# Transposes held back until a group's full-precision products, in a two-layer hybrid decoder

## The chip, the cores and the metric

The kernel runs on one core of a Trainium2 chip, in one launch. The metric is the device time in microseconds, the median of the runs shown. The core has five engines that each work through a queue of their own: TensorE (PE; its weight loads are shown as PEld), VectorE (DVE), ScalarE (ACT), GpSimd (POOL) and SyncE (SP, which here only issues DMAs). Matrix products are written to PSUM, in banks of 128 partitions by 512 fp32 numbers.

## What is computed

A trunk of two layers on 512 tokens with 1024 channels. The parts that matter here:

```
x  <- x + 1/2 SwiGLU_1(RMSNorm(x))
h   = RMSNorm(x)
[q|k|v|z|xBC|dt|g_sb|g_ssm] = h @ W_in
y_sb  = StickBreakingAttention(q,k,v) @ W_branch_sb
y_ssm = Mamba2_SSD(z,xBC,dt) @ W_branch_ssm      # 24 heads x 64 in 8 groups, state 128, chunks of 128
x  <- x + (sigmoid(g_sb)*y_sb + sigmoid(g_ssm)*y_ssm) @ W_out
x  <- x + 1/2 SwiGLU_2(RMSNorm(x))

ssd, per chunk:  cb = c_k b_k^T ;  y = (cb * decay) xdt + c_k state * exp(cum)
                 state <- state * exp(cum_end) + b_k^T (to_end * xdt)
```

## The kernel before, in words

Nearly all of TensorE's work are dense products in which both operands are split into a high and a low part of reduced precision, three matmuls for one (`mm3`, lines 315 to 317). Weights are fetched by SyncE, their high part is cast by ScalarE (line 282), the low part is subtracted by VectorE (line 284), two units ahead of the product that uses them. The dense results rotate through four PSUM banks (pool `pmm`, names `mm`).

The state-space part runs beside the dense products of the mixer. For each of its eight groups, and each of the four chunks c in a group, there are three tasks. `prepare(c)` makes decays on ScalarE (lines 1129 and 1131) and scaled inputs on GpSimd. `inner(c)` multiplies c by b (line 1140) and, except in the last chunk, makes the state's addend (line 1142), both in full precision into a bank of the pool `ptr` (two banks, names `pt`). `outer(c)` multiplies the decayed scores by the inputs (line 1157) and c by the state (line 1159), in full precision into a bank of the pool `pa` (two banks). Inner c+1 and outer c stand together.

The order is written by a clock of ticks: one or two steps of a dense product, of three matmuls each, make a tick, and each task is a generator that runs a step, says how many ticks to sleep, and goes on. What a task issues stands in the engines' queues at that tick. `ssd_group` (from line 1087) starts the chunks `PITCH` = 5 ticks apart.

Blocks have to be transposed between token rows and channel rows. `transposed` (line 849) does three or four 128x128 transposes on TensorE in full precision, each into a quarter of a bank:

- `conv_block` transposes the blocks x (named `cv`) and b (named `bT`) into a bank of `ptr`; ScalarE copies them out (lines 1053 and 1061).
- the end of `ssd_group` transposes the normed result of each group (named `raw`) and, after every second group, a tail of both (named `acc`) into a bank of `pa`; ScalarE takes the high part out (line 1223) and VectorE the low part (line 1225), both named `yt`.

The z products (`by_tokens`, 128x384) fill the four dense banks at once; `z_part` empties each by ScalarE (line 1082) and VectorE (line 1084).

Of the kernel before, what the change touches and what calls it, by code (L numbers as in the profile page):

```python
# [84 lines left out]
def conv_at(kind, i):  # L85

    if kind == "x":
        return OFF_X + i * P, i * TAPS
    at = (OFF_B, OFF_C)[kind == "c"] + i * P
    return at, (DIN // P + GROUPS * (kind == "c") + i) * TAPS  # L90
# [63 lines left out]
def all_units():  # L154
    table, off = {}, 0
    for layer in range(DEPTH):
        for key, n in unit_order(layer):
            table[key] = (off, n)
            if "pair" not in key or key[-1] in STORED:
                off += n * P * P  # L160
    return table, off


class Builder:
# [7 lines left out]
    def __init__(self, ctx, tc, xT, wflat, par, taps, out):  # L172
        self.tc, self.nc = tc, tc.nc
        self.ctx = ctx
        self.xT, self.wflat, self.par, self.taps, self.out = xT, wflat, par, taps, out
        self.units, _ = all_units()
        self.keys = list(self.units)
        self.pos = 0
        self.raw, self.loaded = [], []
        self.count = 0  # L180
        self.side = []
        self.xd = None
        self.sums, self.early, self.summed = {}, {}, 0
        for i, key in enumerate(self.keys):
            if key[2:] == ("gate", 0):
                first = i + 4
            if "pair" in key and key[-1] in ("s1", "s3"):
                self.early.setdefault(max(first, i - (5 if key[-1] == "s1" else 4)), []).append(key)
        self.logs = True

    def name(self, s):
        self.count += 1
        return f"{s}_{self.count}"
# [12 lines left out]
        self.side.append([gen, wait])  # L206

    def tick(self):
        for task in list(self.side):
            task[1] -= 1  # L210
            if task[1] <= 0:
                try:
                    task[1] = next(task[0])
                except StopIteration:
                    self.side.remove(task)
# [573 lines left out]
    def dt_stage(self, layer, ps):  # L789
# [56 lines left out]
        self.give("raw", "raw", "cv", "cv")  # L846
        self.dt_done = True

    def transposed(self, src, n=NT, aside=False):

        pt = self.t(self.pa, [P, SEQ], "pa") if aside else self.t(self.ptr, [P, SEQ], "pt")
        for c in range(n):
            cs = slice(c * P, (c + 1) * P)
            self.nc.tensor.transpose(pt[:, cs], src[:, cs], self.ident)  # L854
        return pt[:, :n * P].rearrange("p (c d) -> p c d", d=P)
# [160 lines left out]
    def conv_block(self, kind, i, ps):  # L1016


        nc, mp = self.nc, self.mp
        r = yield from self.take("raw")  # L1020
        u = yield from self.take("cv")
        _, k0 = conv_at(kind, i)
        tap = [self.conv[:, k0 + j:k0 + j + 1] for j in range(TAPS)]
        nc.scalar.activation(u, ps, AF.Identity, scale=tap[KCONV - 1], bias=tap[KCONV])  # L1024
        yield 2
        for j in range(1, KCONV):
            nc.vector.scalar_tensor_tensor(u[:, j:], ps[:, :SEQ - j], tap[KCONV - 1 - j], u[:, j:],  # L1027
                                           op0=ALU.mult, op1=ALU.add)
            yield 1
        yield 1  # L1030
        yield from self.opened()
        nc.scalar.activation(r, u, AF.Tanh)
        yield 1
        if self.cumb is None:
            self.load_cum(0)
        dst = u
        if kind != "x":
            dst = self.ssm[i][kind] = self.t(mp, [P, SEQ], kind + "T")
        nc.vector.scalar_tensor_tensor(dst, r, 1.0, u, op0=ALU.add, op1=ALU.mult)
        yield 3  # L1040
        if kind == "x":
            p, i = divmod(i, 3)
            pt = self.transposed(dst)
            yield 1
            for g in (2 * p, 2 * p + 1):
                a, b = max(i * P, g % 2 * GW), min((i + 1) * P, (g % 2 + 1) * GW)
                if a < b:
                    if "x" not in self.ssm[g]:
                        while not self.room["xs"]:
                            yield 1  # L1050
                        self.room["xs"] -= 1
                        self.ssm[g]["x"] = self.t(mp, [P, NT, GW], "xs", bufs=3)
                    nc.scalar.activation(self.ssm[g]["x"][:, :, a - g % 2 * GW:b - g % 2 * GW],
                                         pt[:, :, a - i * P:b - i * P], AF.Copy, scale=0.5)
                    self.ssm[g]["x", i] = True
            yield 1
        elif kind == "b":
            pt = self.transposed(dst, NT - 1)
            yield 1
            tok = self.t(mp, [P, NT - 1, P], "btok")  # L1060
            nc.scalar.copy(tok, pt)
            self.ssm[i]["btok"] = tok
        self.give("raw", "cv")
# [28 lines left out]
    def ssd_group(self, layer, g):  # L1092
# [15 lines left out]
        def heads(ap):  # L1108
            return ap.rearrange("p (h d) -> p h d", d=HD)

        def wide(ap):
            return ap.unsqueeze(2).to_broadcast([P, HPG, HD])

        def col(band, c):
            return tok[:, c, 32 * band + h0:32 * band + h0 + HPG]

        def span(c):
            return slice(c * P, (c + 1) * P)

        def prepare(c):  # L1120
            dec = decs[c] = self.t(mp, [P, HPG, P], "dec")
            x = heads(xs[:, c, :])
            if c < NT - 1:
                xws[c] = self.t(mp, [P, HPG, HD], "xw")
                nc.gpsimd.tensor_tensor(xws[c], x, wide(col(3, c)), op=ALU.mult)
            xdts[c] = self.t(mp, [P, HPG, HD], "xdt")
            nc.gpsimd.tensor_tensor(xdts[c], x, wide(col(0, c)), op=ALU.mult)
            for i in range(HPG):
                nc.scalar.activation(dec[:, i, :], cumb[:, i, span(c)], AF.Relu, scale=-1.0,
                                     bias=tok[:, c, 32 + h0 + i:33 + h0 + i])  # L1130
            nc.scalar.activation(dec, dec, AF.Exp, scale=-1.0)
            yield 1
            nc.gpsimd.affine_select(out=dec, in_=dec, pattern=[[0, HPG], [1, P]], compare_op=ALU.is_ge, fill=0.0,
                                    base=0, channel_multiplier=-1)
            nc.gpsimd.tensor_tensor(heads(y[:, c, :]), x, wide(par[:, G_D + h0:G_D + h0 + HPG]), op=ALU.mult)
# [42 lines left out]
            finished.append(c)  # L1178

        self.spawn(prepare(0))  # L1180
        yield 3
        self.spawn(inner(0))
        self.spawn(prepare(1))
        for c in range(NT):
            yield self.PITCH
            if c < NT - 1:
                self.spawn(inner(c + 1))
            self.spawn(outer(c))
            if c + 2 < NT:
                self.spawn(prepare(c + 2), 1)  # L1190
            elif c + 2 == NT and g < GROUPS - 1:
                yield 1
                self.load_cum(g + 1)
# [20 lines left out]
            todo.append((tail, 3 * (g // 2) + 2))  # L1214
        for src, blk in todo:
            yield 4
            pt = self.transposed(src.rearrange("p c d -> p (c d)"), aside=True).rearrange("p c d -> p (c d)")
            if src is yn:
                self.give("raw")
            yield 1  # L1220
            gain = par[:, G_SSM + blk:G_SSM + blk + 1]
            hi, lo = self.pair(self.yt, ("yt", "yt"))
            nc.scalar.activation(hi, pt, AF.Copy, scale=gain)
            yield 1
            nc.vector.scalar_tensor_tensor(lo, pt, gain, hi.bitcast(F32), op0=ALU.mult, op1=ALU.subtract)
            self.y_ssm[blk] = (hi, lo)
# [297 lines left out]
```

## Time and profile before

| | |
|---|---|
| three runs | 2598.34, 2594.51 and 2594.2 us; median 2594.51 |
| profiled execution | 2594.82 us, span 2593.0 us |
| TensorE busy | 2575.7 us (99%), 15074 matmuls |
| VectorE, ScalarE, GpSimd busy | 1761.2 us (68%), 1279.6 us (49%), 492.1 us (19%) |
| chain that ended last | TensorE 93%, VectorE 4%, ScalarE 2% |

The share of TensorE is its modelled busy time; since matmuls overlap, the distance between two starts tells more than the length of a row. A timeline row has the start, the length, the engine, the line, the operation, what it writes and reads and the shape; in brackets stand the idle time of the engine before it and who ended it. A full-precision matmul counts as two instructions there.

### The profile page before, as it was taken

What the parts mean: (1) busy time and instruction counts of PE and PEld (TensorE: products, weight loads), DVE (VectorE), ACT (ScalarE), POOL (GpSimd) and SP (SyncE); (2) the same over time, 40 slices, a digit from 0 to 9 for tenths busy, and PEclk for the clock granted to TensorE, in tenths of its full rate; (3) what the DMA queues carried; (4) which work ended last, traced back from release to release, by engine and by line L of the source; (5) the groups of instructions that cost most, each with busy time, mean ns of one, the idle gap of its engine ahead of it and who ended that gap; (6) DMA issues with size and microseconds to landing.
All of it is one profiled execution on the core that took longest, in us unless ns stands there. A gap on an engine that the chain in (4) does not pass through costs nothing.

```text
span 2593.0 us, 38317 instructions
## 1 busy us (share of the span) xinstructions
PE 2575.7 (99%) x15074; PEld 2300.5 (89%) x15074; DVE 1761.2 (68%) x2422; ACT 1279.6 (49%) x2101; POOL 492.1 (19%) x617
## 2 busy tenths in 40 slices
PE   9999999999999999999999999999999999999998
PEld 7898988888888889899998989888888888899997
DVE  7575876676664478585885858766676644776766
ACT  6343456655554255343553535566555533543444
POOL 0121201133242002021111312011333310021110
PEclk9999999999999999999999999999999999999999
DMA  5455442333333546473554645423333335464642
GB/s 189 137 147 146 122 139 76 102 114 101 109 104 106 163 140 169 131 187 108 161 142 127 173 129 130 137 74 113 101 102 104 113 112 160 139 182 128 175 121 78
DMA packets 105156, 336.35 MB, mean 130 GB/s; under 512 B 12256, under 2 KB 15584, under 8 KB 104976
## 3 DMA queue, kind: packets, MB, share of 16 engines
q1 hardware_dynamic: 93168, 293.46, 35.4%
q0 software_dynamic: 10944, 39.85, 8.7%
q8 instruction: 118, 1.93, 0.3%
q10 hardware_dynamic: 864, 0.60, 0.1%
q14 instruction: 62, 0.51, 0.1%
HBM read 321.18 MB, written 12.68 MB: 129 GB/s over the span
## 4 chain that ended last, share of the span: by engine, by line
PE 93%; DVE 4%; ACT 2%; DMA 1%; issue 1%; SPq 0%; DVEq 0%; ACTq 0%
PE mm L315 26%; PE mm L317 26%; PE mm L316 26%; PE pa L316 3%; PE pa L317 3%; PE pa L315 3%; PE pa L1157 2%; DVE wlo L284 1%; PE pa L1159 1%; PE pt L854 1%; PE pt L1142 1%; DMA wraw<-in_wflat_dram 1%; PE pt L1140 1%; ACT whi L282 1%; PE pa L968 0%
## 5 line engine op out<-in xcount | busy, mean ns | idle before, releaser
L282 ACT CAST whi<-wraw 128x1024 fp32r<-128x1024 f32 (+2 forms) x442 | 435.8, 986 | 604.3 <-PE mm L317 492.0
L284 DVE TENSOR_TENSOR wlo<-wraw,whi 128x1024 fp32r<-128x1024 f32 (+2 forms) x442 | 542.0, 1226 | 168.6 <-ACT whi L282 167.5
L315 PE MATMUL mm<-hhi,whi 128*128 128x512 f32 (+1 forms) x1600 | 571.9, 357 | 0.0
L316 PE MATMUL mm<-hhi,wlo 128*128 128x512 f32 (+1 forms) x1600 | 559.1, 349 | 2.1 <-DVE wlo L284 2.1
L317 PE MATMUL mm<-hlo,whi 128*128 128x512 f32 (+1 forms) x1600 | 559.7, 350 | 0.4 <-DVE hlo L504 0.4
L317 PEld LDWEIGHTS mm<-hlo,whi 128*128 128x128 f32 x1600 | 302.8, 189 | 40.9 <-DVE hlo L504 0.8
L316 PEld LDWEIGHTS mm<-hhi,wlo 128*128 128x128 f32 x1600 | 303.3, 190 | 39.4 <-DVE wlo L284 3.4
L315 PEld LDWEIGHTS mm<-hhi,whi 128*128 128x128 f32 x1600 | 303.2, 190 | 35.8 <-issue 1.0
L617 POOL TENSOR_TENSOR g<-g,rs 128x512 f32<-128x512 f32 x76 | 133.0, 1749 | 876.4 <-DVE g L624 855.4
L284 DVE TENSOR_TENSOR wlo<-s,whi 128x1024 fp32r<-128x1024 f32 x152 | 235.3, 1563 | 58.6 <-ACT whi L282 58.6
L315 PE MATMUL mm<-act,whi 128*128 128x512 f32 (+1 forms) x710 | 274.0, 386 | 0.0
L316 PE MATMUL mm<-act,wlo 128*128 128x512 f32 (+1 forms) x710 | 273.8, 386 | 0.0
L317 PE MATMUL mm<-act,whi 128*128 128x512 f32 (+1 forms) x710 | 273.6, 385 | 0.0
L315 PE MATMUL mm<-th,whi 128*128 128x256 f32 x912 | 258.1, 283 | 0.0
L316 PE MATMUL mm<-th,wlo 128*128 128x256 f32 x912 | 258.1, 283 | 0.0
L317 PE MATMUL mm<-tl,whi 128*128 128x256 f32 x912 | 258.1, 283 | 0.0
L282 ACT CAST whi<-s 128x1024 fp32r<-128x1024 f32 x152 | 158.8, 1045 | 103.3 <-PE mm L317 61.2
L643 DVE SCALAR_TENSOR_TENSOR x<-mm,x 128x512 f32<-128x512 f32 x93 | 64.1, 689 | 196.1 <-PE mm L317 196.1
L315 PEld LDWEIGHTS mm<-th,whi 128*128 128x128 f32 x912 | 175.1, 192 | 0.0
L316 PEld LDWEIGHTS mm<-th,wlo 128*128 128x128 f32 x912 | 175.1, 192 | 0.0
L317 PEld LDWEIGHTS mm<-tl,whi 128*128 128x128 f32 x912 | 175.1, 192 | 0.0
L1027 DVE SCALAR_TENSOR_TENSOR cv<-mm,conv,cv 128x511 f32<-128x511 f32 x168 | 125.1, 744 | 47.9 <-ACT cv L1024 46.3
(297 smaller groups left out, 5030.0 us busy)
## 6 DMA issues: line engine op xcount, KB each, us to landing
wraw<-in_wflat_dram SPq DMA_DIRECT2D x330, 512.0 KB, 3.7
s<-in_wflat_dram SPq DMA_DIRECT2D x76, 512.0 KB, 4.6
s<-in_wflat_dram POOLq DMA_DIRECT2D x76, 512.0 KB, 9.3
wraw<-in_wflat_dram SPq DMA_DIRECT2D x96, 384.0 KB, 3.1
cumb<-cum_d SPq DMA_DIRECT2D x16, 768.0 KB, 4.3
xd<-x SPq DMA_DIRECT2D x16, 256.0 KB, 3.2
wraw<-in_wflat_dram SPq DMA_DIRECT2D x16, 256.0 KB, 3.2
x<-xd SPq DMA_DIRECT2D x16, 256.0 KB, 5.3
```

The lines of the kernel that those rows point to most:

```text
L282: nc.scalar.copy(hi[:, :n], raw[:, :n])
L284: nc.vector.tensor_tensor(lo[:, :n], raw[:, :n], hi[:, :n].bitcast(F32), op=ALU.subtract)
L315: mm(ps, a[0], b[0], start=start, stop=False, **kw)
L316: mm(ps, a[1], b[0], start=False, stop=False, **kw)
L317: mm(ps, a[0], b[1], start=False, stop=stop, **kw)
L617: eng.tensor_tensor(r, r, self.rs[:, cols].unsqueeze(1).to_broadcast([P, 2, half]), op=ALU.mult)
L643: self.nc.vector.scalar_tensor_tensor(x, pd, 0.5, x, op0=ALU.mult, op1=ALU.add)
L854: self.nc.tensor.transpose(pt[:, cs], src[:, cs], self.ident)
L1027: nc.vector.scalar_tensor_tensor(u[:, j:], ps[:, :SEQ - j], tap[KCONV - 1 - j], u[:, j:], op0=ALU.mult, op1=ALU.add)
L1140: nc.tensor.matmul(pc[:, :P], bt[:, span(c)], ct[:, span(c)], start=True, stop=True)
L1142: nc.tensor.matmul(pu, btok[:, c, :], xws[c].rearrange("p h d -> p (h d)"), start=True, stop=True)
L1157: nc.tensor.matmul(py[:, i * HD:(i + 1) * HD], decs[c][:, i, :], xdts[c][:, i, :], start=True, stop=True)
```

## The change

Two methods are added. `due(ticks)` notes the tick at which a group's next full-precision products will be issued; `ssd_group` calls it before each sleep. `together(tag)` holds a task back: as long as a noted tick still lies ahead, it lets one transposing task for each tag (`pt` for the x and b blocks, `pa` for raw and tail) through at a noted tick, in which the products' tasks are later in the list, and makes it sleep otherwise. Where no noted tick lies ahead, it does nothing. The tasks that wait keep their room in the pools.

```diff
+        self.now, self.joined = 0, {}
...
     def tick(self):
+        self.now += 1
...
+    def together(self, tag):
+        while self.joined and self.now < max(self.joined):
+            if tag not in self.joined.get(self.now, (tag,)):
+                self.joined[self.now] += (tag,)
+                return
+            yield 1
+
+    def due(self, ticks):
+        self.joined[self.now + ticks] = ()
...
         if kind == "x":
             p, i = divmod(i, 3)
+            yield from self.together("pt")
             pt = self.transposed(dst)
...
         elif kind == "b":
+            yield from self.together("pt")
             pt = self.transposed(dst, NT - 1)
...
         self.spawn(prepare(0))
+        self.due(4)
         yield 3
         self.spawn(inner(0))
         self.spawn(prepare(1))
         for c in range(NT):
+            self.due(self.PITCH + 1)
             yield self.PITCH
...
         for src, blk in todo:
             yield 4
+            yield from self.together("pa")
             pt = self.transposed(src.rearrange("p c d -> p (c d)"), aside=True).rearrange("p c d -> p (c d)")
```

In the order that comes of it, 18 groups of transposes stand elsewhere on TensorE (one x block, four b blocks, two raw blocks and two tails in each layer), and with them their readers on ScalarE and VectorE; SyncE and GpSimd have the same order as before. The lines of the changed kernel are up to 20 higher.

TensorE before, in the second layer, at the tail of the second pair of groups (`pa_19594`), the second product group behind it (`pt_19608` is inner 1, `pa_19613` outer 0):

```order
L854 MATMUL pa_19594<-ident,acc_19025 128x128 x4
L315 MATMUL mm_19459<-whi_19476,hhi_15893 128x384
L316 MATMUL mm_19459<-whi_19476,hlo_15894 128x384
L317 MATMUL mm_19459<-wlo_19477,hhi_15893 128x384
L1140 MATMUL pt_19608<-cT_19329,bT_19240 128x128
L1142 MATMUL pt_19608<-xw_19562,btok_19291 128x192
L1157 MATMUL pa_19613<-xdt_19522,dec_19519 128x64 x3
```

TensorE after, at the same tail (now `pa_19647`), one product group further on (`pt_19652` is inner 2, `pa_19657` outer 1):

```order
L319 MATMUL mm_19459<-wlo_19539,hhi_15900 128x384
L869 MATMUL pa_19647<-ident,acc_19025 128x128 x4
L1157 MATMUL pt_19652<-cT_19329,bT_19240 128x128
L1159 MATMUL pt_19652<-xw_19610,btok_19327 128x192
L1174 MATMUL pa_19657<-xdt_19560,dec_19557 128x64 x3
L1176 MATMUL pa_19657<-state_19556,cT_19329 128x192
```

The tail has moved past inner 1 and outer 0, and so its `pa` bank is taken after outer 0's and not before.

ScalarE before, from the raw block's copy (`yt_19549`) and the tail's (`yt_19605`) to the first z activation:

```order
L1223 ACTIVATE yt_19549<-pa_19536,par_107 128x512
L1129 ACTIVATE dec_19561<-cumb_19363,sq_16580 128x128 x3
L1131 ACTIVATE dec_19561<-dec_19561 128x384
L282 CAST whi_19599<-wraw_19457 128x1024
L1223 ACTIVATE yt_19605<-pa_19594,par_107 128x512
L1129 ACTIVATE dec_19617<-cumb_19363,sq_16580 128x128 x3
L1131 ACTIVATE dec_19617<-dec_19617 128x384
L1129 ACTIVATE dec_19666<-cumb_19363,sq_16580 128x128 x3
L1131 ACTIVATE dec_19666<-dec_19666 128x384
L282 CAST whi_19673<-wraw_19531 128x1024
L1082 ACTIVATE z_19690<-mm_19459 128x384
```

ScalarE after, the same stretch:

```order
L1146 ACTIVATE dec_19557<-cumb_19363,sq_16580 128x128 x3
L1148 ACTIVATE dec_19557<-dec_19557 128x384
L1243 ACTIVATE yt_19572<-pa_19547,par_107 128x512
L284 CAST whi_19594<-wraw_19457 128x1024
L1146 ACTIVATE dec_19609<-cumb_19363,sq_16580 128x128 x3
L1148 ACTIVATE dec_19609<-dec_19609 128x384
L1146 ACTIVATE dec_19662<-cumb_19363,sq_16580 128x128 x3
L1148 ACTIVATE dec_19662<-dec_19662 128x384
L284 CAST whi_19669<-wraw_19531 128x1024
L1243 ACTIVATE yt_19675<-pa_19647,par_107 128x512
L1099 ACTIVATE z_19690<-mm_19459 128x384
```

The raw block's copy stands behind the decays of chunk 1, and the tail's copy behind the decays of chunks 2 and 3 and a weight cast, directly ahead of the z activations.

VectorE after, from the product that inner 2 feeds to the z products (before, the tail's `yt` stood ahead of inner 1's, and the y, t, weight and z operations followed `state` directly):

```order
L1165 TENSOR_TENSOR dec_19609<-pt_19652,dec_19609 128x384
L1169 TENSOR_TENSOR state_19655<-pt_19652,state_19655 128x192
L1245 SCALAR_TENSOR_TENSOR yt_19676<-pa_19647,par_107,yt_19675 128x512
L1179 TENSOR_TENSOR y_19513<-pa_19657,y_19513 128x192
L1182 TENSOR_TENSOR t_3314_19687<-pa_19657,sq_16580 128x192
L286 TENSOR_TENSOR wlo_19670<-wraw_19531,whi_19669 128x1024
L1101 SCALAR_TENSOR_TENSOR z_19690<-z_19690,mm_19459 128x384
```

VectorE before, the same stretch:

```order
L1148 TENSOR_TENSOR dec_19617<-pt_19656,dec_19617 128x384
L1152 TENSOR_TENSOR state_19659<-pt_19656,state_19659 128x192
L1162 TENSOR_TENSOR y_19513<-pa_19661,y_19513 128x192
L1165 TENSOR_TENSOR t_3314_19687<-pa_19661,sq_16580 128x192
L284 TENSOR_TENSOR wlo_19674<-wraw_19531,whi_19673 128x1024
L1084 SCALAR_TENSOR_TENSOR z_19690<-z_19690,mm_19459 128x384
```

The tail's low half has moved in behind inner 2's state, ahead of outer 1's y and t, the low half of a weight and the z products.

## Rows read from the trace of the kernel before

**Rows 1.** The page, busy us, share of the span and instructions of each engine.

```profile
PE 2575.7 (99%) x15074; PEld 2300.5 (89%) x15074; DVE 1761.2 (68%) x2422; ACT 1279.6 (49%) x2101; POOL 492.1 (19%) x617
```

**Rows 2.** Waits of TensorE at transposes: us in total, times, longest us.

```profile
PE pt L854 <- DVE cv L1039: 1.2, 6, 0.2
```

**Rows 3.** Timeline of TensorE around a lone x block: start us, length us.

```profile
1801.68 0.39 PE L317 MATMUL mm<-hlo,whi 128*128 128x512 f32 x1
1801.91 0.60 PE L854 MATMUL pt<-ident,cv 128*128 128x128 f32 x4
1802.27 0.48 PE L315 MATMUL mm<-hhi,whi 128*128 128x512 f32 x1
...
1802.81 0.40 PE L317 MATMUL mm<-hlo,whi 128*128 128x512 f32 x1
```

**Rows 4.** The same around a raw block that already stands in front of products.

```profile
545.16 0.39 PE L317 MATMUL mm<-hlo,whi 128*128 128x512 f32 x1
...
545.84 0.39 PE L317 MATMUL mm<-hlo,whi 128*128 128x512 f32 x1
546.07 0.60 PE L854 MATMUL pa<-ident,raw 128*128 128x128 f32 x4
...
547.53 0.40 PE L317 MATMUL mm<-hlo,whi 128*128 128x512 f32 x1
```

**Rows 5.** The same around the first two products of a group alone.

```profile
516.19 0.39 PE L317 MATMUL mm<-hlo,whi 128*128 128x512 f32 x1
...
517.42 0.39 PE L317 MATMUL mm<-hlo,whi 128*128 128x512 f32 x1
```

**Rows 6.** TensorE at the tail shown above: its transposes, outer 2, the next unit.

```profile
1952.88 0.60 PE L854 MATMUL pa<-ident,acc 128*128 128x128 f32 x4
...
1963.60 0.78 PE L1157 MATMUL pa<-xdt,dec 128*128 128x64 f32 x6
...
1965.12 0.39 PE L315 MATMUL mm<-hhi,whi 128*128 128x512 f32 x1
```

**Rows 7.** ScalarE in the same stretch.

```profile
1952.39 1.05 ACT L282 CAST whi<-wraw 128x1024 fp32r<-128x1024 f32 x1 [1.88 <-PE mm L316]
1953.52 0.69 ACT L1223 ACTIVATE yt<-pa,par 128x512 fp32r<-128x512 f32 x1
...
1960.07 0.99 ACT L1129 ACTIVATE dec<-cumb,sq 128x128 f32<-128x128 f32 x3 [3.31 <-PE pa L1157]
...
1961.52 1.04 ACT L282 CAST whi<-wraw 128x1024 fp32r<-128x1024 f32 x1
1962.47 1.24 ACT L1082 ACTIVATE z<-mm 128x384 f32<-128x384 f32 x3
```

**Rows 8.** VectorE in the same stretch.

```profile
1954.24 0.75 DVE L1225 SCALAR_TENSOR_TENSOR yt<-pa,par,yt 128x512 fp32r<-128x512 f32 x1 [2.39 <-ACT yt L1223]
1954.91 1.22 DVE L284 TENSOR_TENSOR wlo<-wraw,whi 128x1024 fp32r<-128x1024 f32 x1
...
1961.56 0.34 DVE L1162 TENSOR_TENSOR y<-pa,y 128x192 f32<-128x192 f32 x1
1961.82 0.34 DVE L1165 TENSOR_TENSOR t<-pa,sq 128x192 f32<-128x192 f32 x1
1962.59 1.22 DVE L284 TENSOR_TENSOR wlo<-wraw,whi 128x1024 fp32r<-128x1024 f32 x1 [0.43 <-ACT whi L282]
1963.73 1.01 DVE L1084 SCALAR_TENSOR_TENSOR z<-z,mm 128x384 f32<-128x384 f32 x2
...
1965.13 0.55 DVE L1084 SCALAR_TENSOR_TENSOR z<-z,mm 128x384 f32<-128x384 f32 x1
```

**Rows 9.** ScalarE around the copy of the x block of rows 3.

```profile
1802.55 0.60 ACT L1053 ACTIVATE xs<-pt 128x512 f32<-128x512 f32 x1 [1.02 <-PE pt L854]
...
1806.80 0.52 ACT L1131 ACTIVATE dec<-dec 128x384 f32<-128x384 f32 x1
```

**Rows 10.** TensorE at the next-but-one use of the x block's bank pair.

```profile
1809.07 0.38 PE L1140 MATMUL pt<-cT,bT 128*128 128x128 f32 x2
```

## Prediction, on record before the changed kernel ran

> **What bounds the kernel now.** I read the busy shares first: TensorE is busy for 2575.7 of 2593.0 us, VectorE for 68% and ScalarE for 49% [rows 1]. Only what lengthens or shortens TensorE's own row of work, or makes it wait, moves the end. Next the waits of TensorE: the one kind that a transpose shows is 1.2 us in six waits for VectorE's block (line 1039) [rows 2]. So the transposes hardly wait for their data today, and moving them later cannot win more than those 1.2 us on that side. In the order of the changed kernel these six stand where they were (the column "cv" after "raw", outside any running group), so I count nothing for them.
>
> Then I read the timeline of TensorE around one lone transpose group, around one group that already stands in front of products, and around the two-buffer hand-over that the change rearranges; and the same stretch on ScalarE and VectorE.
>
> **What moves.** The order of SyncE and of GpSimd is unchanged, so every DMA keeps its place. On TensorE 18 groups of transposes change place, nine in each layer: one x block, four B blocks, two "raw" blocks and two "acc" blocks (the tails). Nothing is added or removed: each still issues its three or four transposes. Everything else on TensorE stands in the same row as before. Seven of the nine move past a few dense products into the nearest product group. The two tails go further: the raw block arrives later, the tail follows it at a fixed distance, just misses the second product group, and ends in front of the third.
>
> **Term 1, the joining itself.** A lone group of four: from the last dense product before it (1801.68) to the third after it (1802.81) pass 1.13 us [rows 3]; three dense products without it take 545.84 - 545.16 = 0.68 us [rows 4]. It costs 0.45 us. The first two products of a state-space group alone cost 517.42 - 516.19 - 0.68 = 0.55 us [rows 5]. A group in which four transposes stand directly in front of the same two products exists already: 547.53 - 545.84 - 0.68 = 1.01 us [rows 4]. The two apart cost 0.45 + 0.55 = 1.00. So joining is worth nothing within what these rows resolve (0.01 us), and after each lone group the next few dense products start about 0.01 us late, which a joined group has once and not twice. I bound a move from both sides by +0.02 us (the joined row as it reads, rounded up) and -0.04 us (the slow products after a lone group, four of them by 0.01), and take -0.01: 18 x -0.01 = -0.2 us, with ends at +0.4 and -0.7.
>
> At this place the Trainium skill says something else. "TensorE: Matmul & The Clock Gate", Part 4: PE-mode transpose, gives a transpose some 275 ns in a kernel, of which 173 ns are access latency. Were that latency paid once by each lone group, joining would by that page save an estimated 18 x 0.173 = 3.1 us. The trace does not agree: four transposes start at 1801.91 and the next dense product at 1802.27, so a transpose takes 0.09 us of TensorE and its latency lies under the next one [rows 3]. The 0.60 us of that row is the modelled end of the pipeline and not time that TensorE loses.
>
> **Term 2, the tails and their PSUM bank.** The pool "pa" has two banks, used in turn. Before, the turn is raw, acc, outer 0, outer 1, outer 2, outer 3. After, it is raw, outer 0, acc, outer 1, outer 2, outer 3. So outer 2 (line 1157 of before) now takes the bank out of which the tail has to be read by ScalarE (line 1223) and then VectorE (line 1225). Before, it took outer 0's, long read. The place stands four times with the same spacing, twice in each layer (the tails of the second and of the third pair of groups); I work it out at the third of the four.
>
> The tail's transposes leave 1952.88 and now stand directly in front of the third product group, inner 2 and outer 1; what lies between runs 0.36 us earlier and what follows as before [rows 3, 6]. On ScalarE the tail's copy now stands behind the three decays of the last chunk, which wait for outer 1 and start at 1960.07, their exponential, and the weight cast at 1961.52. It starts where now the z activations start, at 1962.47, and takes 0.69 us: it ends at 1963.16 [rows 7]. VectorE's half follows 0.03 us behind it, as it does now (1953.52 + 0.69, then 1954.24), and takes 0.75 us: 1963.19 to 1963.94 [rows 7, 8]. Outer 2 starts at 1963.60 [rows 6]. TensorE waits 0.34 us.
>
> What is queued behind the waiting VectorE instruction? The y and t operations of outer 1 (0.26 us from start to start, taken for both), the low half of a weight (1.14 us to the next start) and then the z products [rows 8]. VectorE's first z product gives the dense PSUM bank back in which the next unit (the 128x512 product at 1965.12) is built. Its start moves from 1963.73 to 1963.19 + 0.67 (the tail's half, start to start) + 0.26 + 0.26 + 1.14 = 1965.52, and with the 0.55 us of a single one it ends at 1966.07. TensorE wants the bank at 1965.12 [rows 6], so it goes on 0.95 us later than now, and that contains the first wait: TensorE loses 0.95 us at the place, and it has no idle time in which to win it back. Four places: 3.8 us.
>
> Bounds: if the next unit were not waiting for that z product, only the first wait stays, 4 x 0.34 = 1.4 us. If it waited for the second as well, 0.46 us more each (1.01 for the pair less 0.55): 5.6 us. If ScalarE reached the copy early enough, nothing: 0. I take 3.8, since the 128x512 product comes directly behind the fourth z product and the rotation of the four dense banks gives it the first.
>
> That VectorE cannot pass the waiting instruction is to be seen now: its low half at 1954.91 had its cast since 1953.44 (1952.39 + 1.05), but started only after the tail's half, for which VectorE had sat idle 2.39 us [rows 7, 8]. The Trainium skill, "PSUM — Partial Sum Buffer", section Engine vs sequencer instructions, says that ScalarE, VectorE and GpSimd queues are strict FIFO; the row agrees. With a queue that could be passed the second wait would fall away and the change would cost 1.4 - 0.2 = 1.2 us.
>
> **Term 3, the other readers.** The two raw blocks are read in time: their bank is next used two product groups on, by the tail. The x block's copy on ScalarE (0.60 us) moves behind the exponential that ends at 1807.32, so it ends near 1807.9, and its bank is written again at 1809.07 [rows 9, 10]: 1.2 us of cover. The convolution and the cast behind it slide by 0.60 us; both belong to units that are not yet being multiplied. The B blocks' copies sit in the same pattern. I cost all at 0; without that cover the x copy would cost up to its 0.60 us in each layer.
>
> **Sum.** -0.2 + 3.8 + 0 = +3.6 us. The profiled execution took 2594.82 us (2593.0 of span and 1.8 around it) and becomes 2598.4; it lies 0.3 above the median of the runs shown, 2594.51, so I predict 2598.1 us for the median, 0.14% slower. A measurement of this kernel can tell about 0.2%, or 5.2 us, from no change: most likely no change will be found.
>
> **Rivals.**
> - *The cover holds.* ScalarE reaches the tail's copy before the cast, or outer 2 finds its bank free, and only term 1 is left: 2594.3 us. For it: ScalarE is idle for 3.31 us before the last decays [rows 7]. Against: these wait for outer 1 itself, behind which the tail now stands, so the copy cannot use that idle time.
> - *The z products hold two units, slower.* At the same four places the next unit waits for the second z product too, so the price is 0.95 + 0.46 = 1.41 us a place: 5.6 - 0.2 = +5.4, or 2599.9 us. It decides the sign as soon as a place costs over 1.35 us. For it: two z products stand as a pair of 1.01 us behind the same cast, and VectorE falls 1.8 us behind there. Against: each has a bank of its own.
> - *Each lone group pays for its start.* The transposes' row lasts 0.60 us and TensorE goes on after 0.36; if the difference of 0.24 us were lost by each lone group and hidden by joining, 18 x 0.24 = 4.3 us would be won and the tails cost little: 2590.2 us. The joined group in the trace speaks against it, since it costs as much as its parts. This is the mechanism of the skill's page in term 1.
>
> **How the numbers follow.** Forecast 0.60; cover holds 0.19; slower through z 0.16; start-up won 0.05. The range reaches from the covered case with its joining gain (2593.9) to the pair of z products with a little above it (2600.4); it leaves out the start-up case and some of the far slow side. Of the forecast about 0.03 falls above 2599.7 through the scatter of the runs (2594.2 to 2598.34) and of the start-up case 0.03 below 2589.3. That gives faster 0.03, same 0.78, slower 0.19.
>
> **What the profile after would show.** Right: four new waits of TensorE at outer 2 for VectorE's tail copy, about 0.3 to 0.4 us each, and four at the first dense product of the next unit for the z product, about 0.6 each; the joined groups cost the sum of their parts; no wait at the x and B blocks. Wrong: no wait at these places (the cover holds), or one over 1.3 us, or lone groups that turn out dearer than 0.45 us against 1.01 joined.

## The result, and the profile after

The changed kernel takes 2599.52 us (median of 18 executions, 2598.26 to 2601.72), the kernel before, beside it on the same chips, 2595.0 (2593.69 to 2598.34). The ratio is 1.0016 with a 95% interval of 1.0009 to 1.0022: slower by 0.16%, or 4.5 us. That lies below the 0.2% that the prediction took as telling apart, but the interval leaves out 1: the loss is small and real. The forecast was 2598.1 us.

The profiled execution took 2601.24 us, with a span of 2599.5. The busy times of the page stand within 1.3 us of those in [rows 1], but for 2.9 us more on TensorE:

```profile
PE 2578.6 (99%) x15074; PEld 2301.2 (89%) x15074; DVE 1762.5 (68%) x2422; ACT 1278.5 (49%) x2101; POOL 492.9 (19%) x617
```

The waits of TensorE (what waited, for whom, us in total, times, longest us):

```profile
PE mm L318 <- DVE wlo L286: 2.8, 2, 2.2
PE pa L1174 <- DVE yt L1245: 1.3, 4, 0.3
PE pt L869 <- DVE cv L1054: 1.2, 6, 0.2
...
PE mm L317 <- DVE z L1101: 1.1, 4, 0.3
```

The third row is that of [rows 2], unchanged: the transposes wait for VectorE's block as before. The second and the fourth are new and come four times each: outer 2 waits for VectorE's half of the tail, and the first dense product of the next unit waits for a z product. The first is the opening of the kernel and has nothing to do with the change (below).

The timeline of TensorE at the third of the four places, which answers to [rows 6] (times here are later than there by what was lost before; the same products start 4.21 us later at 1940 us):

```profile
1962.47 0.60 PE L869 MATMUL pa<-ident,acc 128*128 128x128 f32 x4
1962.91 0.39 PE L1157 MATMUL pt<-cT,bT 128*128 128x128 f32 x2
...
1967.57 0.38 PE L1157 MATMUL pt<-cT,bT 128*128 128x128 f32 x2
1968.28 0.85 PE L1174 MATMUL pa<-xdt,dec 128*128 128x64 f32 x6 [0.32 <-DVE yt L1245]
...
1969.69 0.33 PE L319 MATMUL mm<-wlo,hhi 128*128 128x384 f32 x1
1970.31 0.50 PE L317 MATMUL mm<-hhi,whi 128*128 128x512 f32 x1 [0.28 <-DVE z L1101]
1970.65 0.40 PE L318 MATMUL mm<-hhi,wlo 128*128 128x512 f32 x1
```

The tail's transposes now stand directly in front of inner 2. Between the row of inner 3 and outer 2 lie 0.71 us from start to start, where 0.22 lay before; the next unit starts 0.62 us behind the last 128x384 product, where it stood 0.18 behind it.

The timeline of ScalarE in the same stretch, answering to [rows 7]:

```profile
1964.27 0.99 ACT L1146 ACTIVATE dec<-cumb,sq 128x128 f32<-128x128 f32 x3 [3.75 <-PE pa L1174]
1965.29 0.53 ACT L1148 ACTIVATE dec<-dec 128x384 f32<-128x384 f32 x1
1965.73 1.04 ACT L284 CAST whi<-wraw 128x1024 fp32r<-128x1024 f32 x1
1966.67 0.68 ACT L1243 ACTIVATE yt<-pa,par 128x512 fp32r<-128x512 f32 x1
1967.24 1.24 ACT L1099 ACTIVATE z<-mm 128x384 f32<-128x384 f32 x3
```

And that of VectorE, answering to [rows 8]:

```profile
1967.38 0.75 DVE L1245 SCALAR_TENSOR_TENSOR yt<-pa,par,yt 128x512 fp32r<-128x512 f32 x1 [1.54 <-ACT yt L1243]
1968.04 0.35 DVE L1179 TENSOR_TENSOR y<-pa,y 128x192 f32<-128x192 f32 x1
1968.31 0.35 DVE L1182 TENSOR_TENSOR t<-pa,sq 128x192 f32<-128x192 f32 x1
1968.57 1.22 DVE L286 TENSOR_TENSOR wlo<-wraw,whi 128x1024 fp32r<-128x1024 f32 x1
1969.71 1.01 DVE L1101 SCALAR_TENSOR_TENSOR z<-z,mm 128x384 f32<-128x384 f32 x2
```

ScalarE has been idle for 3.75 us when outer 1 lets it go; then the decays, the exponential and the cast stand in front of the tail's copy. VectorE's half follows, and behind it y, t, the low half of the weight and the z products come in the order, and with the distances, that the prediction wrote down.

**Where the time went.** The start of a TensorE instruction in the trace after, less the start of the same instruction in the trace before (15074 in both), is a running account: 2.33 us at 60 us, 2.33 at 500, 2.19 at 660, 3.30 at 690, 4.36 at 830, 4.34 at 1780, 4.21 at 1940, 5.33 at 1975, 6.37 at 2110 and at the end. So the two stretches with joined groups and no tail give back 0.14 + 0.13 us, the four places take 1.11, 1.06, 1.12 and 1.04 us, and the change comes to 6.37 - 2.33 = +4.04 us by this trace. The other 2.33 us are there before the first joined group.

These come from the opening. Near 54 us TensorE waits for the low half of a weight, 1.57 us in the profile before (the row below) and 2.2 in the one after (the first row of its waits above), and behind the longer wait the granted clock falls.

```profile
53.88 0.50 PE L316 MATMUL mm<-hhi,wlo 128*128 128x512 f32 x1 [1.57 <-DVE wlo L284]
```

Windows of the kernel after (length, busy time of each engine, granted clock, DMA share, GB/s):

```profile
54.00:56.00 2.00, 1.43 (x5) 1.21 (x6) 1.90 (x5) 1.66 (x3) 0.00 (x0) 0.84 0.19 41
56.00:58.00 2.00, 2.00 (x6) 1.52 (x6) 1.97 (x6) 0.62 (x1) 0.00 (x0) 0.50 0.64 227
58.00:60.00 2.00, 2.00 (x9) 1.59 (x8) 2.00 (x4) 1.93 (x3) 0.00 (x0) 0.81 0.01 2
```

The clock stays at 1.00 there in the profile before. The same difference comes and goes among the experiments' profiles, whose first 60 us are the same work, so it is not the change's.

### The profile page after: what moved, and what is told of

The parts are those of the page before. It is cut to its first block, busy times and chain, and to the rows that moved or that the text cites. A ratio compares the mean times of both kernels' runs of the same rounds, so it can differ in the third digit from the quotient of the medians.

```text
span 2599.5 us, 38319 instructions
## 1 busy us (share of the span) xinstructions
PE 2578.6 (99%) x15074; PEld 2301.2 (89%) x15074; DVE 1762.5 (68%) x2422; ACT 1278.5 (49%) x2101; POOL 492.9 (19%) x617
## 4 chain that ended last, share of the span: by engine, by line
PE 92%; DVE 4%; ACT 2%; DMA 1%; issue 1%; SPq 0%; DVEq 0%; ACTq 0%
PE mm L317 26%; PE mm L319 26%; PE mm L318 26%; PE pa L318 3%; PE pa L319 3%; PE pa L317 3%; PE pa L1174 1%; DVE wlo L286 1%; PE pt L869 1%; ACT whi L284 1%; PE pt L1159 1%; PE pa L1176 1%; DMA wraw<-in_wflat_dram 1%; PE pt L1157 1%; PE pa L983 0%
```

## The experiments

The theory: the tail's copy ends too late in ScalarE's and VectorE's queues; outer 2 must have the bank out of which it reads, and the z product that frees the next unit's bank stands behind it on VectorE. Joining itself is worth a few tenths of a us. The rivals: joining, or a joined row, costs or wins something of its own; one of the two waits is beside the point; the late copy alone is harmless.

All results stand in one table. "Opening" is the running account against the profile before at 60 us; "places" what the account gains at each of the four tails.

| kernel | median us (before) | ratio, 95% interval | opening | places, us |
|---|---|---|---|---|
| after | 2599.52 (2595.0) | 1.0016, 1.0009 to 1.0022 | 2.33 | 1.11, 1.06, 1.12, 1.04 |
| only x and b held back | 2595.11 (2595.39) | 1.0001, 0.9992 to 1.0011 | -0.48 | none |
| only raw and tail held back | 2600.29 (2595.39) | 1.002, 1.0011 to 1.0028 | 0.83 | 1.07, 1.07, 1.07, 1.10 |
| tail not held back | 2595.66 (2595.39) | 1.0, 0.9991 to 1.0008 | 2.84 | none |
| tail's copy a tick sooner | 2595.41 (2595.39) | 0.9999, 0.999 to 1.0007 | 0.08 | none |
| tail's copy a tick later | 2595.47 (2595.28) | 0.9998, 0.9989 to 1.0008 | 3.65 | none |
| tail's copy three ticks later | 2595.25 (2595.28) | 0.9999, 0.9989 to 1.0009 | 2.81 | none |
| tail in the other pool | 2599.46 (2595.57) | 1.0015, 1.0007 to 1.0024 | 0.08 | 1.11, 1.03, 1.12, 1.05 |
| a tick later, banks in turn | 2599.71 (2595.57) | 1.0014, 1.0005 to 1.0023 | 3.20 | 1.09, 1.08, 1.10, 1.08 |
| ScalarE's half twice | 2603.34 (2595.57) | 1.003, 1.0019 to 1.004 | -0.22 | 1.80, 1.77, 3.39, 1.80 |
| ScalarE's half three times | 2608.22 (2595.55) | 1.0047, 1.0031 to 1.0064 | -0.17 | 2.52, 3.68, 2.51, 3.98 |

**Only x and b held back.**

```diff
             yield 4
-            yield from self.together("pa")
             pt = self.transposed(...
```

> Only the x and B blocks are held back (10 of the 18 groups); raw blocks and tails stand as before. Late-copy theory (the loss comes from the four tails alone, whose copy out of PSUM comes late and holds the bank that outer 2 needs): no wait of TensorE at outer 2 or at the next unit, 10 x -0.01 = -0.1 us against before, so no change. Rival, joining is dear (the loss is spread over all 18 joined groups): 10/18 of the 4.5 us, +2.5 us.

None of the new waits is there, and the median is that of the kernel before. The account falls by 0.35 us from 500 to 2110 us: the ten x and b groups that are joined win that and cost nothing.

**Only raw and tail held back.**

```diff
         if kind == "x":
             p, i = divmod(i, 3)
-            yield from self.together("pt")
...
         elif kind == "b":
-            yield from self.together("pt")
```

> Only the raw blocks and the tails are held back (8 of the 18 groups). Late-copy theory: all four pairs of waits are there, about 0.32 us idle at outer 2 and 0.28 at the next unit, 1.05 us a place from start to start, +4.1 us against before. Rival, joining is dear: 8/18 of the 4.5 us, +2.0 us.

All eight waits are there, of 0.31 and 0.28 us, and the places cost what they cost in the changed kernel. The loss belongs to this half of the change.

**Tail not held back.**

```diff
             yield 4
-            yield from self.together("pa")
+            if src is yn:
+                yield from self.together("pa")
```

> All is held back except the tails; the tail still comes after outer 0, so the two banks turn as in the changed kernel, but its copy stands on ScalarE ahead of the last chunk's decays and of the weight cast. Late-copy theory: the bank is free in time, no wait at outer 2 or at the next unit, about -0.2 us against before. Rival, the turn of the banks (outer 2 waits as soon as it follows the tail in the turn, wherever the copy stands): +4 us. Rival, joining is dear: 14/18 of the 4.5 us, +3.5 us.

The raw blocks are held back and the tail is not: the waits are gone. The tail still comes behind outer 0, and the banks of tail, outer 1, outer 2 and outer 3 are those of the changed kernel at all four places, so the bank without a late copy costs nothing. The account falls by 0.35 us between 500 and 2110 us.

**The tail's copy a tick sooner.** TensorE's order is that of the changed kernel, and so are the banks at the four places.

```diff
             if src is yn:
                 self.give("raw")
-            yield 1
+                yield 1
             gain = par[:, G_SSM + blk:G_SSM + blk + 1]
```

> TensorE has the same order as in the changed kernel, all 18 groups joined; only the copies of the tails are issued one tick sooner, ahead of the last chunk's decays and of the weight cast on ScalarE and ahead of inner 2's products on VectorE. Late-copy theory: ScalarE copies during its idle 3.8 us right behind the tail's transposes, so no wait at outer 2 and none at the next unit, about -0.2 us against before and 4.2 us faster than the changed kernel. Rivals, joining is dear or the turn of the banks: +4.5 us against before, as the changed kernel, since TensorE's order and the banks are the same.

The timeline of ScalarE at the same place in that kernel:

```profile
1955.62 0.53 ACT L1148 ACTIVATE dec<-dec 128x384 f32<-128x384 f32 x1
1958.74 0.69 ACT L1243 ACTIVATE yt<-pa,par 128x512 fp32r<-128x512 f32 x1 [2.59 <-PE pa L869]
1959.90 0.99 ACT L1146 ACTIVATE dec<-cumb,sq 128x128 f32<-128x128 f32 x3 [0.48 <-PE pa L1174]
```

The copy now uses the idle time in front of the last decays, and starts 0.64 us after the transposes (1958.10). VectorE's half ends at 1961.40 there, 2.0 us before outer 2 (1963.43). No wait is left, and with it goes the whole loss, although every joined row of TensorE is kept. So the row itself costs nothing; the place of a copy in another engine's queue does.

**The tail's copy a tick later, and three ticks later.** The first was to move the loss to outer 2, the second to make it larger.

```diff
             if src is yn:
                 self.give("raw")
-            yield 1
+            yield 1 if src is yn else 2
             gain = par[:, G_SSM + blk:G_SSM + blk + 1]
```

Both halves of the copy are issued later. At the four places ScalarE's order stays as it is with one tick, and VectorE's half moves behind y, t and the low half of the weight.

> As the changed kernel, with the tails' copies issued one tick later: on ScalarE nothing changes at the four places, on VectorE the tail's half stands behind y, t and the low half of the weight, directly ahead of the z products. One-queue theory (the wait at the next unit comes only from the low half of the weight that stands between the tail's half and the first z product): outer 2 waits longer, the tail's half ends at 1963.73 + 0.75 = 1964.48 on the clock of before, so about 1.0 us from start to start instead of 0.55; the first z product ends near 1964.95 and the next unit, now due near 1966.1, does not wait. The sum per place stays near 1.05 us: +4.0 us against before, no wait at the next unit. Rival, the two waits add up on their own: 1.0 + 0.5 us a place, +6 us, with both waits in the profile.

The second has 4 in the place of 2, which puts VectorE's half behind the first two z products and ScalarE's behind two z activations.

> As the changed kernel, with the tails' copies issued three ticks later: on ScalarE behind two z activations, on VectorE behind the first two z products. One-queue theory: the tail's half runs from 1964.66 to 1965.41 on the clock of before, outer 2 waits near 1.96 us plus the 0.15 us that passed from VectorE's end to TensorE's start in the changed kernel, about 2.0 us a place, and the next unit does not wait: +8 us against before. Rival, the price is that of the changed place and not of the copy's lateness: +4.5 us as the changed kernel.

Theory and rival both missed, in both kernels: there is no new wait in either, and both take the time of the kernel before. The timeline of TensorE at the third place, in the first of the two:

```profile
1966.62 0.38 PE L1157 MATMUL pt<-cT,bT 128*128 128x128 f32 x2
1966.84 0.78 PE L1174 MATMUL pa<-xdt,dec 128*128 128x64 f32 x6
...
1968.36 0.39 PE L317 MATMUL mm<-hhi,whi 128*128 128x512 f32 x1
```

And that of VectorE:

```profile
1964.81 0.34 DVE L1179 TENSOR_TENSOR y<-pa,y 128x192 f32<-128x192 f32 x1
1965.07 0.34 DVE L1182 TENSOR_TENSOR t<-pa,sq 128x192 f32<-128x192 f32 x1
1965.84 1.23 DVE L286 TENSOR_TENSOR wlo<-wraw,whi 128x1024 fp32r<-128x1024 f32 x1 [0.43 <-ACT whi L284]
1966.98 0.74 DVE L1245 SCALAR_TENSOR_TENSOR yt<-pa,par,yt 128x512 fp32r<-128x512 f32 x1
1967.64 1.01 DVE L1101 SCALAR_TENSOR_TENSOR z<-z,mm 128x384 f32<-128x384 f32 x2
```

Outer 2 starts at 1966.84, before the tail's half has even begun to read at 1966.98. It can't have the tail's bank. The banks that the programs assign say the same: at the first of the four places the tail, outer 1, outer 2 and outer 3 stand in banks 4, 5, 4, 5 of the changed kernel, and in 4, 5, 5, 4 of these two. The pool doesn't always deal its two banks in turn, as I had taken it to. What it did fits a choice of the bank whose last reader was issued first, which no run tests by itself: in the changed kernel the tail's half is issued just ahead of outer 1's y and t, here behind them. Nor does the queue cost anything: y, t and the low half now run while VectorE would have sat idle for the copy (1.54 us in the changed kernel), and the first z product ends at 1968.19 (1967.64 + 0.55), before the next unit starts at 1968.36. A new theory follows: it takes a late copy and the tail's bank together.

**The same with the banks in turn.** The order on every engine is that of the kernel with the copy one tick later (the text below counts the two ticks of its `yield`); only the pool is replaced.

```diff
+        if pool is self.pa:
+            self.turn = 1 - self.turn
+            pool = self.pas[self.turn]
         return pool.tile(list(shape), dtype, tag=tag, ...
...
-            yield 1
+            yield 1 if src is yn else 2
...
-        self.pa = enter(tc.tile_pool(name="pa", bufs=2, space=PSUM))
+        self.pas = [enter(tc.tile_pool(name=f"pa{i}", bufs=1, space=PSUM)) for i in range(2)]
+        self.pa, self.turn = self.pas, 1
```

> The kernel with the tail's copy two ticks later, whose order on every engine it keeps, but the pool's two banks are now taken strictly in turn, so that outer 2 gets the tail's bank again. Bank theory (the pool had given outer 2 the bank of outer 1, which is why the later copy was waited for by nobody): outer 2 wanted its bank at 1966.84 and VectorE's half of the tail ends at 1967.72 in that kernel's trace; with 0.15 us of release it starts 1.03 us late at each of the four places, the first z product (end 1968.19) is then in time, so four waits of 0.8 us or more at outer 2, none at the next unit, and 4 x 1.03 - 0.4 = +3.7 us against the kernel before. Rival (the bank is beside the point, a later copy is harmless for another reason): -0.4 us and no wait.

The waits are back, four of 0.87 us at outer 2 and none at the next unit, and each place costs 1.08 to 1.10 us (line numbers are higher by three in this kernel):

```profile
1968.51 0.38 PE L1160 MATMUL pt<-cT,bT 128*128 128x128 f32 x2
1969.76 0.85 PE L1177 MATMUL pa<-xdt,dec 128*128 128x64 f32 x6 [0.87 <-DVE yt L1248]
```

Nothing but the banks of this pool differs from the kernel that lost nothing, so in this order the bank makes the whole loss.

**The tail in the other pool.** Here the bank is taken away and VectorE's queue is left as it is in the changed kernel.

```diff
-            pt = self.transposed(src.rearrange("p c d -> p (c d)"), aside=True).rearrange("p c d -> p (c d)")
+            pt = self.transposed(src.rearrange("p c d -> p (c d)"), aside=src is yn).rearrange("p c d -> p (c d)")
```

> The changed kernel, but the tails' transposes write a bank of the other PSUM pool (the one of the inner products), so no outer product can wait for the tail's copy; the order on every engine is that of the changed kernel. One-queue theory: VectorE's row (tail half, y, t, low half of a weight, z) keeps its times, so the next unit still starts about 1.05 us late at each of the four places and the first wait was contained in that: no wait at outer 2, four waits at the next unit that grow from 0.28 to about 0.8 us, and +4 x 1.05 - 0.3 = +3.9 us against the kernel before. Rival, the two waits add up: with the first gone 4 x 0.5 - 0.3 = +1.7 us. Rival, the bank alone is the cause: -0.3 us and no wait.

The timeline of TensorE at the third place:

```profile
1965.28 0.38 PE L1157 MATMUL pt<-cT,bT 128*128 128x128 f32 x2
1965.50 0.78 PE L1174 MATMUL pa<-xdt,dec 128*128 128x64 f32 x6
...
1968.02 0.50 PE L317 MATMUL mm<-hhi,whi 128*128 128x512 f32 x1 [0.83 <-DVE z L1101]
1968.36 0.40 PE L318 MATMUL mm<-hhi,wlo 128*128 128x512 f32 x1
```

Outer 2 waits for nothing, the next unit waits 0.83 us and no longer 0.28, and the places cost the same as ever. The first wait was contained in the second: taking it away alone wins nothing. So the queue does by itself, at the next unit, what the bank does at outer 2, and the theory of copy and bank together was too narrow. A cure has to serve both: the sooner copy does, and so does the later one, where outer 2 has another bank and y, t and the low half are no longer behind the tail's half.

**ScalarE's half of the tail two and three times.** The copy comes later by a known time and the bank stays.

```diff
-            nc.scalar.activation(hi, pt, AF.Copy, scale=gain)
+            for _ in range(1 if src is yn else 2):
+                nc.scalar.activation(hi, pt, AF.Copy, scale=gain)
```

> The changed kernel with ScalarE's half of every tail done twice, the second time over the same result, and all else in its place: the copy ends 0.58 us later (start to start). One-queue theory: all that stands behind it on VectorE moves by 0.58, so each of the four places costs 1.05 + 0.58 = 1.63 us and the whole is 4 x 1.63 - 0.3 = +6.2 us against the kernel before; the waits at outer 2 grow from 0.32 to about 0.9 and those at the next unit stay near 0.28. Rival, the loss is fixed by the joined row and not by when the copy ends: +3.9 us as in the changed kernel. Rival, only the first wait grows and is made up before the next unit: +3.9 us too, with longer waits at outer 2 and none behind.

Three of the four places cost 1.77 to 1.80 us, 0.72 more than in the changed kernel. I had expected 0.58; but from the first of the two activations to the z activation behind both (1965.53 to 1966.83 in that trace) are 1.30 us, so the second one takes 0.72 and the loss follows it in full. The third place costs 1.6 us more than that, which no theory expected. The timeline of TensorE there:

```profile
1967.86 0.85 PE L1174 MATMUL pa<-xdt,dec 128*128 128x64 f32 x6 [1.03 <-DVE yt L1246]
...
1969.89 0.54 PE L317 MATMUL mm<-hhi,whi 128*128 128x512 f32 x1 [0.28 <-DVE z L1101]
1970.23 0.63 PE L318 MATMUL mm<-hhi,wlo 128*128 128x512 f32 x1
...
1973.22 0.59 PE L319 MATMUL mm<-hlo,whi 128*128 128x512 f32 x1
1973.64 0.39 PE L317 MATMUL mm<-hhi,whi 128*128 128x512 f32 x1
1973.87 0.39 PE L318 MATMUL mm<-hhi,wlo 128*128 128x512 f32 x1
```

From 1970.23 to 1973.64 the products start 0.43 us apart and not 0.23. The windows of that stretch (columns as above) have the granted clock at 0.50, which is 1.2 of 2.4 GHz:

```profile
1971.00:1972.00 1.00, 1.00 (x4) 0.72 (x3) 1.00 (x4) 1.00 (x2) 0.22 (x2) 0.50 0.81 295
1972.00:1973.00 1.00, 1.00 (x4) 0.81 (x3) 0.88 (x2) 0.67 (x3) 0.92 (x2) 0.50 0.35 139
```

The same with three was run to see whether the fall belongs to the waits.

> The changed kernel with ScalarE's half of every tail done three times. In the kernel with two, a repeat put the copy 0.72 us later (1.30 us from the first to the z activation behind both, against 0.58), each of the four places cost 1.78 us, and behind the third of them the granted clock of TensorE fell to 0.5 from about 1970.2 to 1973.6, which cost 1.6 us more. Queue theory alone: 0.72 us more at each place, 4 x 2.5 - 0.3 = +9.7 us against the kernel before, waits at outer 2 of about 1.75 us. Clock theory: the longer wait of TensorE lets the clock fall at more of the places; at all four it costs 4 x 1.6 = 6.4 us more, +16 us in all, at one of four, as before, +11 us. If the fall has nothing to do with the waits: none at these places, +9.7 us.

Two of the places cost 2.5 us, as the queue alone would have it, and two cost 3.68 and 3.98. The timeline of TensorE at the second:

```profile
764.87 0.85 PE L1174 MATMUL pa<-xdt,dec 128*128 128x64 f32 x6 [1.75 <-DVE yt L1246]
...
766.90 0.80 PE L317 MATMUL mm<-hhi,whi 128*128 128x512 f32 x1
767.50 0.63 PE L318 MATMUL mm<-hhi,wlo 128*128 128x512 f32 x1
...
769.56 0.40 PE L317 MATMUL mm<-hhi,whi 128*128 128x512 f32 x1
```

Behind the wait of 1.75 us the 128x512 products come 0.36 to 0.60 us apart, until 769.56. The clock reads 0.50 from 767 to 769 us there, and again from 2057 to 2059 at the fourth place; it stays at 1.00 behind equal waits at the other two. So the fall follows such waits, but not each of them; what picks the places stays open. The whole, +12.7 us between the medians, lies between the 11 and the 16 us that were expected for a fall at one place and at four. In the changed kernel itself, with waits of 0.32 and 0.28 us, the windows of 1966 to 1976 us show 1.00.

## Why the prediction was right

- **What bounds the kernel.** Right: TensorE stays at 99%, and the distances that its waits add at the four places make the loss. The transposes of [rows 2] still wait 1.2 us in six.
- **Term 1, the joining.** Right in kind, a little small in size: -0.2 was forecast for 18 groups. The trace after has -0.27 for the ten x and b groups alone (the other eight lie within the places), and the experiments that lose nothing at the tails have -0.29 to -0.45 between 500 and 2110 us for 10 to 18 joined groups. Kernels with the same order on TensorE differ by 0.15 there. All lie in the bounds of +0.4 to -0.7, so that a joined group costs the sum of its parts, as [rows 3 to 5] had it, to within 0.04 us a group. That -3.1 or -4.3 us could be won at the start of each lone group is refuted by the same runs. What the Trainium skill says on the latency ("TensorE: Matmul & The Clock Gate", Part 4: PE-mode transpose) may hold for one transpose: its some 275 ns agree with the record of a single one in the trace before, which lasts 0.27 us with a modelled end. TensorE's row doesn't lose the latency, neither alone nor joined.
- **Term 2, the chain.** Right: ScalarE's order, VectorE's order, both waits and all four places are as forecast. Set back by the 4.21 us that the place was late, the first z product starts at 1965.50, and 1965.52 was forecast. The first wait lies within the loss at the next unit, as the tail in the other pool shows: no first wait, the same loss.
- **Term 2, the size.** 0.95 us a place were forecast and 1.04 to 1.12 measured. At the third place the next unit starts 1970.31 - 1965.12 - 4.21 = 0.98 us late, since TensorE goes on 0.05 us after the z product's end (1969.71 + 0.55), which I had set to zero. Its first product then takes 0.34 us to the next one, where one that had not waited took 0.23; these 0.11 I had left out, and they are most of what the size is off. At outer 2 the same: 0.34 forecast, 1968.28 - 1963.60 - 4.21 = 0.47 measured, since TensorE starts 0.15 us after VectorE's end (1968.13). The waits forecast were 0.3 to 0.4 us at outer 2 and about 0.6 at the next unit; the first is as forecast (0.32), the second is 0.28, or 0.44 from start to start (0.62 less 0.18). The 0.32 and 0.28 us that the view of waits prints don't add up to the loss; the distance between starts does.
- **Term 2, the banks.** The step says that the pool's banks are used in turn. The two rows of banks that it writes down are true of these two programs, so the sum holds; the rule behind them isn't true, and the expectations of two experiments fell by it. That it held here was luck: had the copy been issued one tick later, it would have failed.
- **Term 3.** Right: no wait at the x and b blocks. ScalarE's copy of the x block stands at 1811.55 for 0.58 us, behind the exponential of [rows 9], as forecast, and its bank is written without a wait as in [rows 10].
- **The sum.** +3.6 forecast; -0.27 and +4.33, rounded, are the +4.04 of the trace; +4.5 between the medians, whose interval, 0.09% to 0.22%, or 2.3 to 5.7 us, holds both. That the rest of the 4.5 is the scatter of the openings is likely, but not shown. The prediction held that a change of this size would not be told from none; 18 executions on either side did tell it.
- **The rivals.** That the cover holds is what the sooner copy makes true; in the changed kernel it isn't, for the reason given (the decays wait for outer 1). That z holds two units is refuted: TensorE goes on as soon as the first z product ends, 0.46 us ahead of the second. The strict order of VectorE's queue, which the Trainium skill states ("PSUM — Partial Sum Buffer", Engine vs sequencer instructions), agrees with every run: with a tail's half that moves 0.72 us, all behind it moves 0.72 us.

## What to carry to other kernels

When a producer is moved later, look first at where its reader then falls in the reader's queue, and what stands behind that reader: here a copy of 0.7 us cost 1.1 us at a bank two operations on, and issuing it one step earlier undid the loss. Where a wait is taken away, ask whether a longer one lies behind it; taking away the bank's wait alone won nothing. Read the bank that each tile really gets instead of counting turns, since a reader that is issued in another order can change it.

## What the runs showed that I had not expected

- The granted clock falls to 0.50 for some 3 us behind a long wait of TensorE. In the twelve profiles' openings, the wait near 54 us lasts 2.17 to 2.23 us in five, all with a granted clock of 0.72 between 54 and 60 us; it lasts 1.26 to 1.99 us in the other seven, and the clock stays at 1.00. In the middle of the kernel it fell behind waits of 1.03 and 1.75 us at three places of eight, so the length of the wait alone doesn't decide it. Between 60 and 2500 us no other fall stands in the twelve profiles. One such fall cost 1.2 to 1.6 us here, more than the wait at some of the places.
- After a wait TensorE's first 128x512 product takes 0.34 us until the next starts, and 0.23 where it did not wait.
- TensorE starts outer 2 0.14 to 0.15 us after the end of the VectorE instruction that it waits for (after: 1968.13 to 1968.28; copy twice: 1967.71 to 1967.86; banks in turn: 1969.62 to 1969.76), where VectorE follows ScalarE's copy within 0.03 us (1967.35 to 1967.38).
